# Attention scores: reciprocal and high part behind the own exponential, low part behind the next maximum; gates behind it too; head norms' first step on GpSimd

## The chip, the cores and the metric

The kernel runs on one core of a Trainium2 chip, as one program. The time is the device time of an execution in microseconds (us); before the change it was 1285.83, 1288.74 and 1289.24 us in three runs, median 1288.74. The profile is of one further execution, recorded by the hardware profiler. Engines are named as the profile names them: PE (TensorE, matrix multiplies; PEld its weight loads), DVE (VectorE), ACT (ScalarE), POOL (GpSimd) and SP (SyncE, which here only issues DMAs; SPq is its queue). L1075 and the like are lines of the kernel.

## The reference

One step of a two-layer model of width 1024 on 256 prompt tokens and 1024 latent tokens. Layer 0 mixes tokens with gated linear attention (GLA), layer 1 with grouped-query attention; the change touches layer 1. Everything is 32-bit.

```
proj = h @ w_in                      # h: modulated rms_norm of x
q, k, v, gate = split(proj)          # 8 query heads, 2 kv heads of 128
q, k = rms_norm(q, qn), rms_norm(k, kn)          # per head: "head norms"
q, k = rope_2d(q), rope_2d(k)                    # latent tokens only
s = q @ k.T * 128 ** -0.5            # latents see 1024 + 256 cached keys, the prompt its own 256
p = softmax(s)                       # maximum, exponential, divide by the sum
o = p @ v
y = (o * silu(gate)) @ w_out
x = x + gt * y
```

## The kernel before

**Number format.** Products of 32-bit values are made on PE from fp16 pairs: each operand is scaled by a power of two and split into a high part (the value rounded to fp16) and a low part (the rest), and `mm3` (L132) issues three matmuls for a product: high x high, high x low, low x high. So each matrix that goes into a product takes two elementwise passes, one for each part.

**Stages.** Of the profiled span of 1282 us the GLA layer takes the first 620 or so; until about 735 follows its output projection, with the second layer's norm, keys (`key_tile`) and first queries; `attention` runs until about 1180, and `att_out`, the last projection, ends the program.

**Attention.** `steps` holds ten tiles (p, c): kv half p (four query heads each) and a block c of 256 tokens; c = 0 is the prompt with 256 keys, c = 1 to 4 are latent blocks with 1280 keys. A tile has four heads and each head two scores j = 0, 1 of 128 queries, so there are 80 scores, 64 of them against 1280 keys. `scores` issues, for one score: the matmuls S (L1072, PE, into one of two PSUM tiles), the maximum smx (L1075, DVE), its scaled negative snb (L1077, ACT), and the exponential p with the sum sden beside it (L1080, ACT). `rest` turns p into what PE takes: the reciprocal srec of the sum (L1096, DVE), the same scaled, srec2 (L1098, DVE), the high part of p divided by the sum (L1101, POOL, "hi" below), the low part (L1102, DVE, "lo"), both in a tile phl, and a DMA transpose phl to PT (L1103, issued on SP). `values` multiplies PT with the values two heads later (L132, mm<-PT,vh and mm<-PT,vl), then multiplies by the gate (L1126, DVE, qk) and stores. Beside the scores, `query` and `query_rest` make the queries of coming tiles, one projection in every two heads: `head_norm` squares and sums on ACT (L919, hssq), then `rstd` takes hrsa = hssq/128 + eps (L121, DVE) and its power -1/2, hrs (L123, POOL), and DVE multiplies (L922); `rope` is eight POOL multiplies (L933) and two of DVE (L935, L936); a split and a DMA transpose follow (L946, L947, L950). `gateT` makes the gates of two heads: a projection on PE and silu, which is a tanh on ACT (ls, L275) and one DVE operation (gx, L277).

**Order.** A scheduler orders each engine's instructions by a simulated run before the program is built; on the chip each engine works through its list in that order. `issue_after(x)` makes what is issued under it come behind instruction x in that order. Before the change `scores` ends with `rest(last)`: the whole `rest` of the score before, all of reciprocal, hi, lo and transpose, is issued behind the maximum of the score just issued.

**Buffers.** p and phl have two buffers each, PT three, S two. So hi of a score waits until the transpose has read phl of two scores before, and an exponential waits until lo has read p of two scores before.

**End of attention.** Behind the last scores the output row of the first block, OUT[0], is brought back (`out2_load`) and split (`out2_prep`: two maxima L1211, a power of two by way of PE, then four splits L1218, L1219), the gate vector is folded into the output weights (L799, POOL), the first output tile is issued (`out_tile`), and the last two heads' `values` come last. `att_out` does the same for the other four blocks.

Of the kernel before, what the change touches and what calls it, by code (L numbers as in the profile page):

```python
# [7 lines left out]
F16 = mybir.dt.float16  # L8
F32 = mybir.dt.float32
# [3 lines left out]
ALU = mybir.AluOpType  # L13
# [4 lines left out]
P = 128  # L18
D = 1024
KT = D // P  # L20
TP, TS = 256, 1024
# [3 lines left out]
PAST = 256  # L25
GH, DK, DV, RANK = 4, 128, 256, 16
GQ, GV = GH * DK, GH * DV
HD, AH, KVH = 128, 8, 2
EPS = 1e-6
# [19 lines left out]
OUT = (1, 0, 2, 3, 4)  # L49
# [8 lines left out]
class K:  # L58
# [55 lines left out]
        return o  # L114


    def rstd(self, ssq, n, tag):
        nc = self.nc
        w = ssq.shape[1]
        a = self.t(self.sm, [P, w], F32, tag + "a")  # L120
        nc.vector.tensor_scalar(a, ssq, 1.0 / n, EPS, ALU.mult, ALU.add)  # L121
        r = self.t(self.sm, [P, w], F32, tag)
        nc.gpsimd.tensor_tensor(r, a, self.mhalf[:, 0:w], ALU.pow)  # L123
        return r
# [788 lines left out]
    def head_norm(self, x, g, out):  # L913
        nc = self.nc
        n = x.shape[1]
        ssq = self.t(self.sm, [P, n], F32, "hssq")
        junk = self.t(self.hw, [P, HD], F32, "hjunk", bufs=1)
        for j in range(n):
            nc.scalar.activation(junk, x[:, j, :], AF.Square, accum_out=ssq[:, j : j + 1])  # L919
        r = self.rstd(ssq, HD, "hrs")  # L920
        for j in range(n):
            nc.vector.scalar_tensor_tensor(out[:, j, :], x[:, j, :], r[:, j : j + 1], g, ALU.mult, ALU.mult)  # L922

# [134 lines left out]

    def scores(self, h, c, j, q, PT):
        nc = self.nc  # L1060
        kv = h // (AH // KVH)
        nk = 256 if c == 0 else TS + PAST
        k0 = 10 * P if c == 0 else 0
        S = (self.S0 or self.t(self.ps, [P, 1536], F32, "S"))[:, 0:nk]
        self.S0 = None
        qh, ql = (q[:, h % 4 // 2, m, h % 2, :] for m in range(2))
        a = 0
        while a < nk:
            n = min(512, nk - a)
            kh, kl = (t[:, kv, k0 + a : k0 + a + n] for t in (self.kTh, self.kTl))  # L1070
            for m, (x, y) in enumerate(((qh, kh), (qh, kl), (ql, kh))):
                nc.tensor.matmul(S[:, a : a + n], x, y, start=m == 0, stop=m == 2)  # L1072
            a += n
        mx = self.t(self.sm, [P, 1], F32, "smx")
        last = nc.vector.tensor_reduce(mx, S, AX.X, ALU.max).ins  # L1075
        nb = self.t(self.sm, [P, 1], F32, "snb")
        nc.scalar.activation(nb, mx, AF.Copy, scale=self.nsexp)  # L1077
        p = self.t(self.sp, [P, TS + PAST], F32, "p")[:, 0:nk]
        den = self.t(self.sm, [P, 1], F32, "sden")
        nc.scalar.activation(p, S, AF.Exp, scale=self.sexp, bias=nb, accum_out=den)  # L1080
        self.rest(last)
        self.last = last
        self.put_off = p, den, PT, j, nk


    def rest(self, after=None):
        if self.put_off is None:
            return
        if after is not None:
            with self.tc.issue_after(after):  # L1090
                return self.rest()
        nc = self.nc
        p, den, PT, j, nk = self.put_off
        self.put_off = None
        r = self.t(self.sm, [P, 1], F32, "srec")
        nc.vector.reciprocal(r, den)  # L1096
        r2 = self.t(self.sm, [P, 1], F32, "srec2")
        nc.vector.tensor_scalar(r2, r, 2.0 ** 14, None, ALU.mult)  # L1098
        parts = self.t(self.sp, [P, 2 * (TS + PAST)], F16, "phl")[:, 0 : 2 * nk]
        hi, lo = parts[:, 0:nk], parts[:, nk:]  # L1100
        nc.gpsimd.tensor_scalar(hi, p, r, 2.0 ** 14, ALU.mult, ALU.mult)  # L1101
        nc.vector.scalar_tensor_tensor(lo, p, r2, hi, ALU.mult, ALU.subtract)  # L1102
        nc.sync.dma_start_transpose(PT[:, 0 : 2 * nk // P, j * P : j * P + P], parts)  # L1103


    def gateT(self, h, c, w, inv):
# [2 lines left out]
        ps = self.bank("mm")[:, 0:256]  # L1109
        self.mm3(ps, lambda k: (hi[:, k, g0 : g0 + HD], lo[:, k, g0 : g0 + HD]), lambda k: self.hT(k, 256 * c, 256))  # L1110
        half, inv = inv[h % 4 // 2]
        return self.silu_raw(ps, half, 256), inv

    def values(self, h, c, PT, g):
        nc = self.nc
# [41 lines left out]
    def attention(self, wo):  # L1157
# [3 lines left out]
        for n, (p, c) in enumerate(self.steps):  # L1161
# [6 lines left out]
            for e in range(4):  # L1168
                h = 4 * p + e
                if later:  # L1170
                    self.nc.sync.dma_start(*later.pop(0))
                PT = self.t(self.sp, [P, 20, 256], F16, "PT", bufs=3)
                self.scores(h, c, 0, q[(p, c, 0)], PT)
                if e % 2 == 0:
                    self.query()
# [19 lines left out]
        self.fold_gate(1, o0[2] + [inv for _, inv in self.o1], gt)  # L1195
        wo[:] = [(*o0[0:2], 512)] + [(*w, 256) for w, _ in self.o1]
        self.out_tile(OUT[0], 0, self.t(self.sp, [P, TS + PAST], F32, "p")[:, 0:D], wo)
        for t in pend:
            self.values(*t, g.pop(t[0]))

# [3 lines left out]
        return og  # L1204

    def out2_prep(self, og, parts):
        nc = self.nc
        hi, lo = parts
        mx = self.t(self.small, [P, 2], F32, "wmx")
        for j in range(2):  # L1210
            nc.vector.tensor_reduce(  # L1211
# [1 line left out]
            )  # L1213
        m = self.t(self.small, [P, 1], F32, "wm1")
        nc.vector.tensor_tensor(m, mx[:, 0:1], mx[:, 1:2], ALU.max)
        s, inv = self.pow2(m)
        for k in range(0, AH, 4):
            nc.scalar.activation(hi[:, k : k + 4], og[:, k : k + 4], AF.Copy, scale=s)  # L1218
            nc.vector.scalar_tensor_tensor(  # L1219
# [15 lines left out]
    def att_out(self, wo):  # L1235
        w = self.wtile(2)
        for n, c in enumerate(OUT):
            if n + 1 < 5:
                nxt = self.out2_prep(self.out2_load(OUT[n + 1]), [t[:, :, 256 * (n % 2) : 256 * (n % 2) + 256] for t in w[0:2]])
            for j in range(n == 0, 2):  # L1240
                x = self.t(self.xp, [P, D], F32, "xr")
                self.out_tile(c, j, x, wo, (512, 256, 256) if (n, j) == (4, 1) else (512, 512))
# [353 lines left out]
```

## Time and profile before

| what | us |
|---|---|
| runs | 1285.83, 1288.74, 1289.24 (median 1288.74) |
| profiled execution, whole | 1284.12 |
| profiled execution, span | 1282.3 |
| PE busy in the span | 1212.2 |
| DVE / ACT / POOL busy | 895.1 / 584.8 / 389.2 |
| PE busy from 735 to 1180 (attention) | 428.37 of 445 |
| DVE busy from 735 to 1180 | 327.95 of 445 |

The profiled execution is its own run: its time, 1284.12, is 4.6 us under the median, and the 1.8 us between it and the span lie around the recorded work. A row of a stretch ("740.00:760.00 20.00, 18.79 (x118) ...") gives a stretch of the span, its length, the busy time of PE, PEld, DVE, ACT and POOL with the number of instructions, the clock that PE was granted (1.00 is full), the share of the DMA engines and GB/s. A row of the timeline gives start, duration, engine, line, operation, and output<-input; in brackets the time that the engine stood idle just before and what released it. A row of waits gives what waited, for what, us in all, how often, and the longest.

### The profile page before, as it was taken

To read this page: it belongs to the slowest core of one execution; us is meant where nothing else is said; L and a number is where in the kernel's file an instruction comes from. 1 tells how busy PE (TensorE), PEld (TensorE's weight loads), DVE (VectorE), ACT (ScalarE), POOL (GpSimd) and SP (SyncE) were. 2 spreads that over 40 slices of the span, in tenths; PEclk is the share of its full clock that TensorE was granted. 3 is DMA by queue.
4 is the path that set the end of the run, shared out by engine and by line. 5 is a ranking of instruction groups with operands and counts; after the bars stand their busy time and mean duration, and the time that the engine had idled before them with its cause. 6 is when DMAs were issued, how large, how long until landed. Compare 5 with 4: busy or idle time off the path is not lost. (4 is left out here: it accounts for less than half of the span.)

```text
span 1282.3 us, 22586 instructions
## 1 busy us (share of the span) xinstructions
PE 1212.2 (95%) x8295; PEld 810.6 (63%) x8295; DVE 895.1 (70%) x2072; ACT 584.8 (46%) x1425; POOL 389.2 (30%) x617
## 2 busy tenths in 40 slices
PE   4799999999999988999899999999999999999998
PEld 2347666655565545667578757677666766766675
DVE  5645876776688888764487678877667587875652
ACT  3546555555476566420265554444445454441110
POOL 0222222332233324300034545453233245522000
PEclk9899999999999999999999999999999999999999
DMA  9511363653444436994933367768848647768532
GB/s 362 194 66 39 128 198 123 191 164 104 128 135 136 123 111 207 281 206 150 296 131 109 64 142 141 143 125 152 190 107 169 138 91 145 137 133 207 185 130 84
DMA packets 333792, 194.41 MB, mean 152 GB/s; under 512 B 229663, under 2 KB 318607, under 8 KB 332401
## 3 DMA queue, kind: packets, MB, share of 16 engines
q1 hardware_dynamic: 291616, 159.02, 49.0%
q10 hardware_dynamic: 42064, 33.95, 8.6%
q8 instruction: 65, 1.06, 0.3%
q14 instruction: 47, 0.38, 0.1%
HBM read 103.00 MB, written 33.83 MB: 107 GB/s over the span
## 5 line engine op out<-in xcount | busy, mean ns | idle before, releaser
L132 PEld LDWEIGHTS <-hT_hi 128*128 128x128 f16 x1920 | 187.4, 98 | 126.6 <-issue 12.7
L132 PE MATMUL mm<-whi,hT_hi 128*128 128x512 f16 (+1 forms) x560 | 195.5, 349 | 4.0 <-ACT gx L541 2.8
L132 PE MATMUL mm<-wlo,hT_hi 128*128 128x512 f16 (+1 forms) x560 | 195.6, 349 | 0.0
L132 PE MATMUL mm<-whi,hT_lo 128*128 128x512 f16 (+1 forms) x560 | 195.4, 349 | 0.0
L132 PEld LDWEIGHTS <-whi 128*128 128x128 f16 x1408 | 137.9, 98 | 59.0 <-issue 6.2
L132 PE MATMUL mm<-hT_hi,whi 128*128 128x256 f16 (+1 forms) x512 | 153.4, 302 | 3.5 <-POOL hT_hi L416 2.9
L1101 POOL TENSOR_SCALAR phl<-p,srec 128x1280 f16<-128x1280 f32 (+1 forms) x80 | 99.8, 1248 | 186.5 <-DVE srec L1096 119.9
L132 PE MATMUL mm<-hT_lo,whi 128*128 128x256 f16 (+1 forms) x512 | 153.9, 301 | 0.2 <-DVE hT_lo L417 0.2
L132 PE MATMUL mm<-hT_hi,wlo 128*128 128x256 f16 (+1 forms) x512 | 153.7, 301 | 0.0
L1102 DVE SCALAR_TENSOR_TENSOR phl<-p,srec,phl 128x1280 f16<-128x1280 f32 (+1 forms) x80 | 107.6, 1345 | 49.7 <-POOL phl L1101 49.4
L132 PEld LDWEIGHTS <-hT_lo 128*128 128x128 f16 x960 | 94.3, 98 | 62.8 <-issue 1.9
L1072 PE MATMUL S<-kT,wst 128*128 128x512 f16 (+1 forms) x624 | 121.5, 338 | 5.0 <-ACT p L1080 5.0
L132 PE MATMUL mm<-PT,vh 128*128 128x256 f16 x672 | 114.3, 275 | 11.3 <-DMA PT<-phl 8.8
L1080 ACT ACTIVATE p<-S,snb,sexp 128x1280 f32<-128x1280 f32 (+1 forms) x80 | 99.7, 1247 | 30.2 <-DVE srec L1096 10.7
L1075 DVE TENSOR_REDUCE smx<-S 128x1 f32<-128x1280 f32 (+1 forms) x80 | 101.6, 1269 | 16.7 <-PE S L1072 16.7
L1072 PEld LDWEIGHTS <-wst 128*128 128x128 f16 x624 | 61.0, 98 | 56.7 <-issue 5.7
L132 PE MATMUL mm<-PT,vl 128*128 128x256 f16 x336 | 92.4, 275 | 0.0
L132 PEld LDWEIGHTS <-wlo 128*128 128x128 f16 x704 | 69.1, 98 | 29.9 <-issue 1.4
L1077 ACT ACTIVATE snb<-smx,nsexp 128x1 f32<-128x1 f32 x80 | 23.4, 293 | 133.1 <-DVE smx L1075 127.8
L132 PEld LDWEIGHTS <-vh 128*128 128x128 f16 x672 | 65.6, 99 | 23.0 <-issue 10.4
L933 POOL TENSOR_TENSOR rope<-hx,ropet 128x64 f32<-128x64 f32 x160 | 70.3, 468 | 9.2 <-DVE hx L936 5.6
L154 DVE TENSOR_REDUCE wmx<-wst 128x1 f32<-128x512 f32 x96 | 60.4, 676 | 9.0 <-DMA wst<-in_gla_w_in 5.7
(353 smaller groups left out, 2500.9 us busy)
## 6 DMA issues: line engine op xcount, KB each, us to landing
wada<-in_w_ada SPq DMA_DIRECT2D x13, 1024.0 KB
wst<-in_gla_w_in SPq DMA_DIRECT2D x12, 1024.0 KB
wst<-in_att_w_in SPq DMA_DIRECT2D x10, 1024.0 KB
xr<-x_d SPq DMA_DIRECT2D x15, 512.0 KB
og_d<-qk ACTq DMA_DIRECT2D x40, 128.0 KB
wst<-og_d SPq DMA_DIRECT2D x5, 1024.0 KB
out<-xr ACTq DMA_DIRECT2D x17, 256.0 KB
x<-in_x_sample SPq DMA_DIRECT2D x8, 512.0 KB
```

Source lines behind the costliest of these rows:

```text
L132: self.nc.tensor.matmul(out, a, b, start=k == 0 and j == 0, stop=k == n - 1 and j == 2)
L154: nc.vector.tensor_reduce(mx[:, j : j + 1], st[:, 2 * j : 2 * j + 2, :], AX.XY, ALU.max, apply_absolute_value=True)
L933: nc.gpsimd.tensor_tensor(tv[:, h, :, w, :], xv[:, h, :, 1 - w, :], sn[:, :, w, :], ALU.mult)
L1072: nc.tensor.matmul(S[:, a : a + n], x, y, start=m == 0, stop=m == 2)
L1075: last = nc.vector.tensor_reduce(mx, S, AX.X, ALU.max).ins
L1077: nc.scalar.activation(nb, mx, AF.Copy, scale=self.nsexp)
L1080: nc.scalar.activation(p, S, AF.Exp, scale=self.sexp, bias=nb, accum_out=den)
L1101: nc.gpsimd.tensor_scalar(hi, p, r, 2.0 ** 14, ALU.mult, ALU.mult)
L1102: nc.vector.scalar_tensor_tensor(lo, p, r2, hi, ALU.mult, ALU.subtract)
```

## The change

Four things change.

1. `rstd` takes an engine; `head_norm` has its first step (hrsa, L121) done on GpSimd, in all 50 head norms.
2. `rest` is cut in two. The new `high` issues reciprocal, srec2 and hi, and is called at the end of `scores` for the score's own p, with no `issue_after`; `rest`, still behind the next maximum, issues lo and the transpose alone. The last tile (n = 9, `tail`) keeps the old order: there `rest` calls `high` first.
3. In `gateT` the silu is issued behind the last maximum (`issue_after(self.last)`).
4. `out2_prep` is cut in `out2_scale` (maxima and power of two) and `out2_parts` (splits). The second block's row, OUT[1], is loaded and scaled in `attention` ahead of the last two heads' `values`; before, that was done in `att_out`.

```diff
--- before.py
+++ after.py
@@ -114,11 +114,11 @@
         return o
 
 
-    def rstd(self, ssq, n, tag):
+    def rstd(self, ssq, n, tag, eng=None):
         nc = self.nc
         w = ssq.shape[1]
         a = self.t(self.sm, [P, w], F32, tag + "a")
-        nc.vector.tensor_scalar(a, ssq, 1.0 / n, EPS, ALU.mult, ALU.add)
+        (eng or nc.vector).tensor_scalar(a, ssq, 1.0 / n, EPS, ALU.mult, ALU.add)
         r = self.t(self.sm, [P, w], F32, tag)
         nc.gpsimd.tensor_tensor(r, a, self.mhalf[:, 0:w], ALU.pow)
         return r
@@ -917,7 +917,7 @@
         junk = self.t(self.hw, [P, HD], F32, "hjunk", bufs=1)
         for j in range(n):
             nc.scalar.activation(junk, x[:, j, :], AF.Square, accum_out=ssq[:, j : j + 1])
-        r = self.rstd(ssq, HD, "hrs")
+        r = self.rstd(ssq, HD, "hrs", nc.gpsimd)
         for j in range(n):
             nc.vector.scalar_tensor_tensor(out[:, j, :], x[:, j, :], r[:, j : j + 1], g, ALU.mult, ALU.mult)
 
@@ -1081,6 +1081,20 @@
         self.rest(last)
         self.last = last
         self.put_off = p, den, PT, j, nk
+        if not self.tail:
+            self.high()
+
+
+    def high(self):
+        nc = self.nc
+        p, den, *to, nk = self.put_off
+        r = self.t(self.sm, [P, 1], F32, "srec")
+        nc.vector.reciprocal(r, den)
+        r2 = self.t(self.sm, [P, 1], F32, "srec2")
+        nc.vector.tensor_scalar(r2, r, 2.0 ** 14, None, ALU.mult)
+        parts = self.t(self.sp, [P, 2 * (TS + PAST)], F16, "phl")[:, 0 : 2 * nk]
+        nc.gpsimd.tensor_scalar(parts[:, 0:nk], p, r, 2.0 ** 14, ALU.mult, ALU.mult)
+        self.put_off = p, r2, parts, *to, nk
 
 
     def rest(self, after=None):
@@ -1090,15 +1104,11 @@
             with self.tc.issue_after(after):
                 return self.rest()
         nc = self.nc
-        p, den, PT, j, nk = self.put_off
+        if len(self.put_off) == 5:
+            self.high()
+        p, r2, parts, PT, j, nk = self.put_off
         self.put_off = None
-        r = self.t(self.sm, [P, 1], F32, "srec")
-        nc.vector.reciprocal(r, den)
-        r2 = self.t(self.sm, [P, 1], F32, "srec2")
-        nc.vector.tensor_scalar(r2, r, 2.0 ** 14, None, ALU.mult)
-        parts = self.t(self.sp, [P, 2 * (TS + PAST)], F16, "phl")[:, 0 : 2 * nk]
         hi, lo = parts[:, 0:nk], parts[:, nk:]
-        nc.gpsimd.tensor_scalar(hi, p, r, 2.0 ** 14, ALU.mult, ALU.mult)
         nc.vector.scalar_tensor_tensor(lo, p, r2, hi, ALU.mult, ALU.subtract)
         nc.sync.dma_start_transpose(PT[:, 0 : 2 * nk // P, j * P : j * P + P], parts)
 
@@ -1109,7 +1119,8 @@
         ps = self.bank("mm")[:, 0:256]
         self.mm3(ps, lambda k: (hi[:, k, g0 : g0 + HD], lo[:, k, g0 : g0 + HD]), lambda k: self.hT(k, 256 * c, 256))
         half, inv = inv[h % 4 // 2]
-        return self.silu_raw(ps, half, 256), inv
+        with self.tc.issue_after(self.last):
+            return self.silu_raw(ps, half, 256), inv
 
     def values(self, h, c, PT, g):
         nc = self.nc
@@ -1170,6 +1181,7 @@
                 if later:
                     self.nc.sync.dma_start(*later.pop(0))
                 PT = self.t(self.sp, [P, 20, 256], F16, "PT", bufs=3)
+                self.tail = n == len(self.steps) - 1
                 self.scores(h, c, 0, q[(p, c, 0)], PT)
                 if e % 2 == 0:
                     self.query()
@@ -1195,6 +1207,8 @@
         self.fold_gate(1, o0[2] + [inv for _, inv in self.o1], gt)
         wo[:] = [(*o0[0:2], 512)] + [(*w, 256) for w, _ in self.o1]
         self.out_tile(OUT[0], 0, self.t(self.sp, [P, TS + PAST], F32, "p")[:, 0:D], wo)
+        row = self.out2_load(OUT[1])
+        self.second = row, *self.out2_scale(row)
         for t in pend:
             self.values(*t, g.pop(t[0]))
 
@@ -1204,8 +1218,10 @@
         return og
 
     def out2_prep(self, og, parts):
-        nc = self.nc
-        hi, lo = parts
+        return self.out2_parts(og, *self.out2_scale(og), parts)
+
+    def out2_scale(self, og):
+        nc = self.nc
         mx = self.t(self.small, [P, 2], F32, "wmx")
         for j in range(2):
             nc.vector.tensor_reduce(
@@ -1213,7 +1229,11 @@
             )
         m = self.t(self.small, [P, 1], F32, "wm1")
         nc.vector.tensor_tensor(m, mx[:, 0:1], mx[:, 1:2], ALU.max)
-        s, inv = self.pow2(m)
+        return self.pow2(m)
+
+    def out2_parts(self, og, s, inv, parts):
+        nc = self.nc
+        hi, lo = parts
         for k in range(0, AH, 4):
             nc.scalar.activation(hi[:, k : k + 4], og[:, k : k + 4], AF.Copy, scale=s)
             nc.vector.scalar_tensor_tensor(
@@ -1236,7 +1256,8 @@
         w = self.wtile(2)
         for n, c in enumerate(OUT):
             if n + 1 < 5:
-                nxt = self.out2_prep(self.out2_load(OUT[n + 1]), [t[:, :, 256 * (n % 2) : 256 * (n % 2) + 256] for t in w[0:2]])
+                to = [t[:, :, 256 * (n % 2) : 256 * (n % 2) + 256] for t in w[0:2]]
+                nxt = self.out2_prep(self.out2_load(OUT[n + 1]), to) if n else self.out2_parts(*self.second, to)
             for j in range(n == 0, 2):
                 x = self.t(self.xp, [P, D], F32, "xr")
                 self.out_tile(c, j, x, wo, (512, 256, 256) if (n, j) == (4, 1) else (512, 512))
```

On DVE, around two maxima in the middle of attention (the first maximum of each listing is of the same score: S_10375 before is S_10381 of the change; the number in a name is only a count). Before:

```order
L1075 TENSOR_REDUCE smx_10385<-S_10375 128x1
L1096 RECIPROCAL srec_10392<-sden_10306 128x1
L1098 TENSOR_SCALAR srec_2404_10394<-srec_10392 128x1
L1102 SCALAR_TENSOR_TENSOR phl_10396<-p_10305,srec_2404_10394,phl_10396 128x1280
L121 TENSOR_SCALAR hrsa_10432<-hssq_10428 128x2
L1075 TENSOR_REDUCE smx_10459<-S_10449 128x1
L1096 RECIPROCAL srec_10466<-sden_10390 128x1
L121 TENSOR_SCALAR hrsa_10537<-hssq_10533 128x2
L922 SCALAR_TENSOR_TENSOR hx_2406_10400<-hx_2406_10400,hrs_10434,qn_7570 128x128 x2
L1098 TENSOR_SCALAR srec_2420_10468<-srec_10466 128x1
L1102 SCALAR_TENSOR_TENSOR phl_10470<-p_10389,srec_2420_10468,phl_10470 128x1280
```

With the change:

```order
L1075 TENSOR_REDUCE smx_10391<-S_10381 128x1
L1112 SCALAR_TENSOR_TENSOR phl_10320<-p_10311,srec_2392_10318,phl_10320 128x1280
L1092 RECIPROCAL srec_10400<-sden_10396 128x1
L1094 TENSOR_SCALAR srec_2407_10402<-srec_10400 128x1
L1075 TENSOR_REDUCE smx_10465<-S_10455 128x1
L1112 SCALAR_TENSOR_TENSOR phl_10404<-p_10395,srec_2407_10402,phl_10404 128x1280
L922 SCALAR_TENSOR_TENSOR hx_2409_10406<-hx_2409_10406,hrs_10440,qn_7570 128x128 x2
L922 SCALAR_TENSOR_TENSOR hx_2409_10406<-hx_2409_10406,hrs_10545,qn_7570 128x128 x2
L1137 SCALAR_TENSOR_TENSOR qk_7_82<-mm_10480,inv_g_2054_8506,gx_10349 128x256
L1092 RECIPROCAL srec_10474<-sden_10470 128x1
```

Before, every maximum has a reciprocal and srec2 of the score before behind it and then that score's lo; two hrsa lie between. With the change lo stands directly behind the maximum, its reciprocal came ahead of that maximum, and behind lo stands the reciprocal of the score whose maximum was just taken: srec_10400 belongs to smx_10391. The reciprocal of the next score, srec_10474, has a low part, four hx and one qk ahead of it.

On POOL at the same place, before:

```order
L1101 TENSOR_SCALAR phl_10396<-p_10305,srec_10392 128x1280
L123 TENSOR_TENSOR hrs_10434<-hrsa_10432,mhalf_85 128x2
L1101 TENSOR_SCALAR phl_10470<-p_10389,srec_10466 128x1280
L123 TENSOR_TENSOR hrs_10539<-hrsa_10537,mhalf_85 128x2
L933 TENSOR_TENSOR rope_10438<-hx_2406_10400,ropet_7568 128x2x32 x4
L1101 TENSOR_SCALAR phl_10529<-p_10463,srec_10525 128x1280
```

With the change:

```order
L1096 TENSOR_SCALAR phl_10404<-p_10395,srec_10400 128x1280
L121 TENSOR_SCALAR hrsa_10438<-hssq_10434 128x2
L123 TENSOR_TENSOR hrs_10440<-hrsa_10438,mhalf_85 128x2
L121 TENSOR_SCALAR hrsa_10543<-hssq_10539 128x2
L123 TENSOR_TENSOR hrs_10545<-hrsa_10543,mhalf_85 128x2
L933 TENSOR_TENSOR rope_10444<-hx_2409_10406,ropet_7568 128x2x32 x4
L1096 TENSOR_SCALAR phl_10478<-p_10469,srec_10474 128x1280
```

The two hrs of a query projection stood apart with a hi between them; now both stand behind the hi, each with its hrsa directly ahead, and all four ahead of the first rope.

On DVE at the entry to the last tile (smx_14205 before is smx_14211 of the change: the first score of tile n = 9). Before:

```order
L1075 TENSOR_REDUCE smx_14205<-S_14195 128x1
L1096 RECIPROCAL srec_14212<-sden_14126 128x1
L1098 TENSOR_SCALAR srec_3188_14214<-srec_14212 128x1
L1075 TENSOR_REDUCE smx_14230<-S_14220 128x1
L1102 SCALAR_TENSOR_TENSOR phl_14216<-p_14125,srec_3188_14214,phl_14216 128x1280
L1096 RECIPROCAL srec_14237<-sden_14210 128x1
L1126 SCALAR_TENSOR_TENSOR qk_7_82<-mm_14245,inv_g_2622_11538,gx_14163 128x256
```

With the change:

```order
L1075 TENSOR_REDUCE smx_14211<-S_14201 128x1
L1112 SCALAR_TENSOR_TENSOR phl_14140<-p_14131,srec_3176_14138,phl_14140 128x1280
L1075 TENSOR_REDUCE smx_14230<-S_14220 128x1
L1092 RECIPROCAL srec_14237<-sden_14216 128x1
L1094 TENSOR_SCALAR srec_3196_14239<-srec_14237 128x1
L1137 SCALAR_TENSOR_TENSOR qk_7_82<-mm_14245,inv_g_2625_11544,gx_14169 128x256
L1112 SCALAR_TENSOR_TENSOR phl_14241<-p_14215,srec_3196_14239,phl_14241 128x1280
```

Before, the low part of tile 8's last score (phl_14216) stood behind two maxima of tile 9 and behind its own reciprocal; now it stands behind one maximum (phl_14140), and its reciprocal has gone ahead of that. From the second score of the tile on the old order holds.

## The prediction

> **What bounds the kernel now.** I read the work by stretches first, then what PE waits for in attention, then the timeline at those waits, and the groups of instructions for durations. A row of a stretch has start:end, length, then PE, PEld, DVE, ACT and POOL busy, PE's clock, DMA share and GB/s.
>
> ```profile
> 735.00:1180.00 445.00, 428.37 (x3060) 299.18 (x3058) 327.95 (x624) 203.62 (x509) 186.06 (x238) 1.00 0.73 145
> 820.00:840.00 20.00, 20.00 (x139) 13.33 (x138) 15.20 (x26) 10.65 (x26) 10.21 (x11) 1.00 0.71 138
> 840.00:860.00 20.00, 20.00 (x145) 13.92 (x143) 16.07 (x27) 8.96 (x23) 8.83 (x12) 1.00 0.72 142
> ```
>
> In attention, the stage changed, PE is busy for 428.37 of 445 us. In the body of a run of tiles it has no gap: 20.00 of 20.00. So the change can give back only what PE idles, 445 - 428.37 = 16.6 us, and that lies in a few stretches:
>
> ```profile
> 740.00:760.00 20.00, 18.79 (x118) 11.35 (x117) 15.91 (x29) 11.27 (x27) 11.19 (x14) 1.00 0.54 113
> 760.00:780.00 20.00, 16.86 (x131) 12.51 (x130) 16.66 (x31) 10.49 (x25) 11.62 (x14) 1.00 0.80 148
> 920.00:940.00 20.00, 17.37 (x137) 13.08 (x135) 11.28 (x34) 7.50 (x26) 7.22 (x14) 1.00 0.80 155
> 980.00:1000.00 20.00, 18.17 (x145) 14.01 (x144) 15.28 (x30) 11.19 (x27) 6.94 (x6) 1.00 0.86 160
> 1000.00:1020.00 20.00, 19.48 (x150) 14.40 (x149) 11.49 (x35) 8.34 (x29) 7.71 (x15) 1.00 0.66 133
> 1060.00:1080.00 20.00, 18.34 (x133) 12.60 (x131) 17.11 (x32) 9.59 (x22) 11.60 (x14) 1.00 0.81 149
> 1120.00:1140.00 20.00, 17.02 (x115) 11.77 (x113) 17.57 (x24) 9.45 (x17) 6.50 (x5) 0.91 0.74 146
> 1140.00:1160.00 20.00, 17.62 (x139) 13.21 (x138) 15.36 (x26) 8.94 (x16) 4.20 (x4) 1.00 0.78 147
> ```
>
> PE's idle time by these rows: start of attention 1.21 + 3.14 = 4.35; change to the prompt tile (920) 2.63; start of the second half (980 to 1020) 1.83 + 0.52 = 2.35; 1060 1.66; the last tile 2.98 + 2.38 = 5.36. Together 16.35 of the 16.6. What ends these waits:
>
> ```profile
> PE mm L132 <- DMA PT<-phl: 8.8, 7, 2.6
> PE S L1072 <- ACT p L1080: 5.0, 4, 1.8
> PE mm L132 <- DVE ropet L1219: 2.4, 1, 2.4
> DVE phl L1102 <- POOL phl L1101: 49.4, 48, 3.3
> POOL phl L1101 <- DVE srec L1096: 119.9, 38, 6.2
> ```
>
> PE waits for a score's transposed parts (8.8 us) or for the exponential that frees its PSUM tile (5.0). Both stand at the end of one chain: maximum, exponential, reciprocal, hi, lo, transpose. The last two rows show the loose link: POOL stands 119.9 us waiting for a reciprocal that DVE issues only behind the next maximum, and then DVE stands 49.4 us waiting for POOL. That is time of DVE and POOL, and costs only where PE waits.
>
> **The change part by part.** *Reciprocal, srec2 and hi behind the own exponential.* Nothing is removed: each score keeps its six steps. What moves shows best at the last tile's entry:
>
> ```profile
> 1124.15 1.48 DVE L1075 TENSOR_REDUCE smx<-S 128x1 f32<-128x1280 f32 x1
> 1125.55 0.15 DVE L1096 RECIPROCAL srec<-sden 128x1 f32<-128x1 f32 x1
> 1125.85 1.33 POOL L1101 TENSOR_SCALAR phl<-p,srec 128x1280 f16<-128x1280 f32 x1 [4.36 <-DVE srec L1096]
> 1127.89 1.54 DVE L1102 SCALAR_TENSOR_TENSOR phl<-p,srec,phl 128x1280 f16<-128x1280 f32 x1
> 1129.46 3.39 SPq L1103 DMA_TRANSPOSE PT<-phl  x1
> 1131.11 1.78 PE L1072 MATMUL S<-kT,wst 128*128 128x512 f16 x9 [0.64 <-ACT p L1080]
> 1134.97 0.38 PE L132 MATMUL mm<-PT,vh 128*128 128x256 f16 x2 [2.07 <-DMA PT<-phl]
> 1135.00:1138.00 3.00, 3.00 (x20) 2.37 (x21) 3.00 (x3) 0.33 (x3) 1.32 (x1) 0.70 1.09 204
> 1138.00:1141.00 3.00, 3.00 (x23) 2.38 (x20) 1.57 (x6) 1.51 (x2) 1.33 (x1) 0.73 0.54 49
> ```
>
> POOL was free for 4.36 us before its reciprocal came. With the change hi is done by then, and lo can start where the reciprocal stood, at 1125.55 instead of 1127.89: the transpose is issued 1127.89 - 1125.55 = 2.3 us earlier, which covers the wait of 2.07 and pulls the exponentials behind it. Behind that wait PE's clock shows 0.70 and 0.73 for 3 us each: 3 x 0.30 + 3 x 0.27 = 1.7 us of work lost though PE counts as busy. I take the tile's recovery as 4 of its 5.36 (about 1.1 stays: from its second score on the old order holds) and 1.5 of the clock.
>
> [...] This case's trace shows the dip just behind the wait.
>
> The other places:
>
> ```profile
> 917.12 5.62 SPq L1103 DMA_TRANSPOSE PT<-phl  x1
> 924.98 1.33 POOL L1101 TENSOR_SCALAR phl<-p,srec 128x1280 f16<-128x1280 f32 x1 [6.14 <-DMA PT<-phl]
> 926.35 1.55 DVE L1102 SCALAR_TENSOR_TENSOR phl<-p,srec,phl 128x1280 f16<-128x1280 f32 x1 [3.32 <-POOL phl L1101]
> 933.07 0.38 PE L132 MATMUL mm<-PT,vh 128*128 128x256 f16 x2 [2.63 <-DMA PT<-phl]
> ```
>
> At 924.98 hi does not wait for a reciprocal, but 6.14 us for a phl buffer, held by a transpose of 5.62 us that shares the DMA engines with the gate weights. But the scores ahead of it were two steps late too: each gives up its hi of 1.33 between maximum and lo, so the transpose of 917 starts at least 1.33 earlier, and the next follows. Bounds 0 (the transpose is set by the traffic) and 2.63; I take 2.0, nearer the upper end, since the shift comes before the traffic. The clock of the stretch stayed at 1.00 (row of 920), so nothing of a clock is counted here.
>
> At 980 to 1020 weight loads make the transposes slow in the same way: bounds 0 and 2.35, taken 1.5. At 1060: bounds 0 and 1.66; in the same stretch DVE is busy for 17.11 of 20, the fullest of the body, so I take 0.5. At the start (4.35) the first three waits belong to scores with nothing ahead of them, and the new order puts four hx ahead of the third reciprocal: bounds 0 and 3, taken 1.5. The body of the tiles gives nothing, since PE is full there. Sum: 5.5 + 2.0 + 1.5 + 0.5 + 1.5 = 11.0.
>
> *What the early reciprocal costs.* DVE works in order, so a reciprocal whose sum is not there holds back the maximum behind it.
>
> ```profile
> L1102 DVE SCALAR_TENSOR_TENSOR phl<-p,srec,phl 128x1280 f16<-128x1280 f32 x64 | 99.7, 1557 | 46.2 <-POOL phl L1101 46.0
> L1077 ACT ACTIVATE snb<-smx,nsexp 128x1 f32<-128x1 f32 x80 | 23.4, 293 | 133.1 <-DVE smx L1075 127.8 <-DVE srec L1096 5.3
> 1126.04 1.42 ACT L1080 ACTIVATE p<-S,snb,sexp 128x1280 f32<-128x1280 f32 x1
> 1127.35 0.19 ACT L1080 ACTIVATION_READ_ACCUMULATOR p<-S,snb,sexp 128x1 f32 x1
> L936 DVE TENSOR_TENSOR hx<-hx,rope 128x256 f32<-128x256 f32 x28 | 20.6, 735 | 0.0
> L121 DVE TENSOR_SCALAR hrsa<-hssq 128x2 f32<-128x2 f32 x38 | 6.3, 168 | 27.8 <-ACT hjunk L919 27.8
> ```
>
> From maximum to sum it is 0.29 + 1.42 + 0.19 = 1.90 us on ACT; lo covers 1.56 of it, so at most 0.34 us is lost in each score that has no more between. Against that DVE no longer waits for hi: 49.4 us over 80 scores is 0.62 each. I take 0 in the body.
>
> *Head norms.* In attention 38 hrsa leave DVE, 38 x 0.168 = 6.3 us, and the 27.8 us that DVE stood ahead of them. On POOL none is seen; bounds from the nearest rows:
>
> ```profile
> L588 POOL COPY eb<-ep 128x4 f32<-128x4 f32 x40 | 13.3, 332 | 18.4 <-ACT ep L582 17.6 <-ACT ls L560 0.5
> L123 POOL TENSOR_TENSOR hrs<-hrsa,mhalf 128x2 f32<-128x2 f32 x50 | 37.1, 744 | 72.6 <-DVE hrsa L121 72.4
> ```
>
> Between 0.33 and 0.74 us; 0.4, since it is a plain multiply and add like the copy. 38 x 0.4 = 15 us on an engine that has 445 - 186 free. POOL's wait for the squares now holds hi behind it, up to 0.7 us a norm; lo is not due until the next maximum. I allow 1 us over the kernel, and 1 us at the end, where the second block's row (maxima and power of two) now stands on DVE ahead of the last two lo's; that it saves work in `att_out` gives nothing, PE being full there. *Gates behind the maximum:* they move two DVE operations of 0.4 us behind maxima: 0, as long as their PSUM tile is not wanted sooner.
>
> The sum: 11 - 2 = 9 us. The profiled execution goes from 1284.1 to 1275; the median stands 4.6 above that execution, so 1288.7 - 9 = 1280.
>
> **The rivals.** *The transitions stay.* At 924.98 POOL waits for a transpose, not for a reciprocal; if traffic sets all waits up to 1100, only part of the last tile is won, 0 to 3.8 us: about 1287. For it: five of the seven places have weight loads running beside them. Against: at 1125 the chain is plainly late by its order. *All is won.* 14 us and more, up to 16.6 + 1.7 = 18.3: 1271 to 1274. Against it: the start, and the old order in the last tile.
>
> *DVE becomes the bound: slower.* Mechanism: in the body, per two heads, DVE's operations and its waits for the exponential must fit in PE's period.
>
> ```profile
> 800.00 1.48 DVE L1075 TENSOR_REDUCE smx<-S 128x1 f32<-128x1280 f32 x1
> 823.46 1.48 DVE L1075 TENSOR_REDUCE smx<-S 128x1 f32<-128x1280 f32 x1
> 825.36 1.44 DVE L936 TENSOR_TENSOR hx<-hx,rope 128x256 f32<-128x256 f32 x1
> ```
>
> The two maxima are a period of 23.46 us apart (four scores and a query projection). DVE is busy for 15.20 to 16.07 of 20 us in the body, so for 17.8 to 18.9 of a period; about 5 us are free, 1.25 a score. Lost would be up to 0.34 a score for the exponential, and what hi beside DVE costs: L936 takes 0.735 in the mean and 1.44 here, beside POOL; if every operation with two tiles in SBUF (lo above all, 1.56) stretched by as much as L936 does, 0.7, the loss would be 1.04 and the body still fit. It decides from 1.25; with 0.2 us over that on 60 scores it is 12 us, less 5.5 won at the end: about 1295. For it: hi now runs beside DVE's work, where before DVE stood waiting for it. Against it: lo's mean is 1.557, beside the 1.54 and 1.55 of the rows above, so the long operation is not stretched today.
>
> [...]
>
> **How the numbers follow.** Forecast, 4 to 14 us won: 0.58, range 1275 to 1285. Transitions stay: 0.22. All won: 0.06. DVE the bound: 0.14. A measurement here tells about 0.3% from no change, 3.9 us: faster is below 1284.9, slower above 1292.6. Faster is 0.58 + 0.06 = 0.64; same 0.22; slower 0.14. The range 1271 to 1291 takes in all won and transitions that stay, and leaves out the slower case and what lies beyond the bounds.
>
> **What would show it.** Right: PE's idle time from 735 to 1180 falls from 16.6 to about 6; DVE's wait for POOL's hi falls from 49.4 to below 15; no wait of PE for PT over 1 us at the last tile's entry, and no dip of the clock behind it; the body stays at 20.00 of 20. Hrsa on POOL shows about 0.4 us. Wrong: gaps of PE in the body ended by the exponential (DVE the bound); the waits at 760, 933 and 990 unchanged (traffic); new waits of PE at 1150 to 1180, behind the second row's maxima.

## The result and the profile after

The changed kernel takes 1279.49 us in the median of ten runs, 1276.43 to 1286.28; beside it the kernel before took 1288.88, 1285.83 to 1291.97. The ratio is 0.994 with a 95% interval of 0.9922 to 0.9958: 7.7 us faster by the ratio, 9.4 by the medians. Run again beside other kernels it gave 0.9952 (0.9934 to 0.9969), so 6 to 8 us is the fair size. Of all runs here one, of e5 below, was slow: 1590.46 us; it is in that row's median and not in its ratio.

The profiled execution spans 1277.5 us, 4.8 less than the 1282.3 before. The stretches of attention, in the same order as before (start:end, length, PE, PEld, DVE, ACT and POOL busy, PE's clock, DMA share, GB/s):

```profile
735.00:1180.00 445.00, 435.73 (x3129) 304.97 (x3128) 326.58 (x601) 208.69 (x518) 206.48 (x283) 1.00 0.75 150
740.00:760.00 20.00, 17.77 (x113) 10.88 (x112) 13.66 (x23) 11.41 (x32) 10.26 (x15) 1.00 0.54 132
760.00:780.00 20.00, 18.18 (x125) 11.95 (x124) 17.36 (x30) 10.33 (x25) 12.49 (x19) 1.00 0.83 152
920.00:940.00 20.00, 20.00 (x162) 15.64 (x160) 10.79 (x26) 7.78 (x25) 7.74 (x15) 1.00 0.80 138
980.00:1000.00 20.00, 19.89 (x154) 14.85 (x153) 14.64 (x26) 10.89 (x25) 8.96 (x9) 1.00 0.99 172
1060.00:1080.00 20.00, 19.82 (x141) 13.46 (x140) 16.25 (x29) 8.79 (x18) 11.93 (x17) 1.00 0.81 156
1120.00:1140.00 20.00, 19.43 (x148) 14.11 (x147) 18.09 (x26) 8.59 (x17) 5.33 (x4) 1.00 0.67 129
1140.00:1160.00 20.00, 18.73 (x151) 14.43 (x150) 15.40 (x26) 9.90 (x16) 12.14 (x11) 1.00 0.96 218
1160.00:1180.00 20.00, 18.32 (x127) 12.03 (x125) 10.66 (x20) 2.66 (x3) 2.91 (x2) 1.00 0.89 219
```

PE's idle time in attention falls from 16.6 to 445 - 435.73 = 9.3 us. Counted from the first maximum to the last, which lie elsewhere in the two executions, it falls from 416.33 - 399.88 = 16.5 to 408.27 - 400.68 = 7.6 us. At 920 it is gone (2.63 to 0), at 980 nearly so (1.83 to 0.11), at 1060 too (1.66 to 0.18), and in 1120 to 1160 it falls from 5.36 to 1.84. At the start it stays: 2.23 + 1.82 = 4.05, after 4.35. And 1.68 us appear at 1160 to 1180, where there were none: behind the last maximum PE now waits 0.7 us for a PT and 1.0 us for the first output tile (p, L811).

PE's waits there, and the row of all maxima after and before (first and last start):

```profile
PE S L1072 <- ACT p L1080: 4.1, 4, 1.3
PE mm L132 <- DVE gx L277: 1.3, 1, 1.3
PE mm L132 <- DMA PT<-phl: 1.1, 2, 0.7
PE S L132 <- DVE p L811: 1.0, 1, 1.0
...
L1075 DVE TENSOR_REDUCE smx<-S x80: 410/1480/1492, 744.9 to 1153.2; 128x1 f32<-128x1280 f32 x64, 128x1 f32<-128x256 f32 x16
```

```profile
L1075 DVE TENSOR_REDUCE smx<-S x80: 407/1479/1493, 741.1 to 1157.4; 128x1 f32<-128x1280 f32 x64, 128x1 f32<-128x256 f32 x16
```

The waits for PT fell from 8.8 to 1.1 us; those for the exponential from 5.0 to 4.1 only. From the first maximum to the last it was 1157.4 - 741.1 = 416.3 us and is 1153.2 - 744.9 = 408.3: 8.0 us won in attention. That the span shows 4.8 is because attention begins 3.8 us later. Most of that lies ahead of the change, as the last matmuls of the GLA layer show, before and after:

```profile
L673 PE MATMUL U<-Sc,qe x10: 379/380/454, 503.5 to 600.2; 128*128 128x256 f32 x10
```

```profile
L673 PE MATMUL U<-Sc,qe x10: 379/380/382, 507.8 to 603.5; 128*128 128x256 f32 x10
```

They start 3.3 us apart in a stage that the change does not touch. In the other profiles below this stage ends anywhere from 599.7 to 606.3; the profiled execution before was one of the quick ones. So places are compared by distances within attention, not by the spans.

### The profile page after: what moved, and what is told of

Its sections match the earlier page's. It is cut to its first block, busy times and chain, and to the rows that moved or that the text cites. A ratio compares the mean times of both kernels' runs of the same rounds, so it can differ in the third digit from the quotient of the medians.

```text
span 1277.5 us, 22607 instructions
## 1 busy us (share of the span) xinstructions
PE 1210.1 (95%) x8295; PEld 808.3 (63%) x8295; DVE 884.7 (69%) x2022; ACT 585.3 (46%) x1425; POOL 410.0 (32%) x667
## 5 line engine op out<-in xcount | busy, mean ns | idle before, releaser
L1096 POOL TENSOR_SCALAR phl<-p,srec 128x1280 f16<-128x1280 f32 (+1 forms) x80 | 104.1, 1301 | 174.3 <-DVE srec L1092 95.4
L1075 DVE TENSOR_REDUCE smx<-S 128x1 f32<-128x1280 f32 (+1 forms) x80 | 101.6, 1271 | 44.3 <-PE S L1072 44.0
L1112 DVE SCALAR_TENSOR_TENSOR phl<-p,srec,phl 128x1280 f16<-128x1280 f32 (+1 forms) x80 | 106.7, 1333 | 23.6 <-POOL phl L1096 23.5
L1080 ACT ACTIVATE p<-S,snb,sexp 128x1280 f32<-128x1280 f32 (+1 forms) x80 | 99.7, 1246 | 13.3 <-DVE phl L1112 5.2
L1077 ACT ACTIVATE snb<-smx,nsexp 128x1 f32<-128x1 f32 x80 | 23.5, 293 | 116.6 <-DVE smx L1075 116.0
L933 POOL TENSOR_TENSOR rope<-hx,ropet 128x64 f32<-128x64 f32 x160 | 65.3, 436 | 19.1 <-DVE hx L936 10.5
L416 POOL TENSOR_SCALAR hT_hi<-h 128x256 f16<-128x256 f32 (+1 forms) x64 | 36.4, 577 | 96.2 <-ACT h L415 95.7
```

Source lines behind the costliest of these rows:

```text
L416: nc.gpsimd.tensor_scalar(hi, h, 1.0, 1.0, ALU.mult, ALU.mult)
L933: nc.gpsimd.tensor_tensor(tv[:, h, :, w, :], xv[:, h, :, 1 - w, :], sn[:, :, w, :], ALU.mult)
L1096: nc.gpsimd.tensor_scalar(parts[:, 0:nk], p, r, 2.0 ** 14, ALU.mult, ALU.mult)
```

## The experiments

All are edits of the changed kernel unless they say otherwise. "us" is the median; the ratio is to the kernel before, run beside it.

| run | us | ratio, 95% interval | first to last maximum | last maximum to end |
|---|---|---|---|---|
| before | | | 416.3 | 124.9 |
| changed | 1279.49 | 0.9940 (0.9922 to 0.9958) | 408.3 | 124.3 |
| e8, changed again | 1282.02 | 0.9952 (0.9934 to 0.9969) | 408.7 | 125.1 |
| e1, without early reciprocal and hi | 1290.55 | 1.0009 (0.9988 to 1.0030) | 418.4 | 124.5 |
| e2, early reciprocal and hi alone | 1287.65 | 0.9994 (0.9972 to 1.0016) | 409.7 | 127.7 |
| e3, head norms on DVE | 1283.76 | 0.9958 (0.9934 to 0.9983) | 409.8 | 125.3 |
| e4, gates free | 1280.44 | 0.9943 (0.9919 to 0.9967) | 409.9 | 125.7 |
| e5, second row late | 1285.33 | 0.9966 (0.9944 to 0.9987) | 409.0 | 131.0 |
| e6, no old order in the last tile | 1282.75 | 0.9952 (0.9930 to 0.9974) | 408.9 | 127.0 |
| e7a, DVE +0.67 us a score | 1297.93 | 1.0078 (1.0053 to 1.0104) | 422.5 | 126.0 |
| e7b, DVE +1.20 us a score | 1303.08 | 1.0115 (1.0087 to 1.0144) | 433.4 | 124.2 |
| e9, early reciprocal and second row | 1283.14 | 0.9964 (0.9944 to 0.9984) | 409.7 | 125.9 |
| e10, srec2 on POOL | 1281.29 | 0.9946 (0.9925 to 0.9967) | 411.2 | 121.0 |

The last two columns are of one profiled execution each. How many matmuls are left behind the last maximum depends on the order too (862 before, 842 in the changed kernel, 830 in e10), so the sum of the two columns is firmer than each: 541.2 before, 532.6 changed, 537.4 in e2, 535.6 in e9, 540.0 in e5.

**e1: without the early reciprocal**, all tiles in the old order:

```diff
-        if not self.tail:
-            self.high()
```

> The changed kernel, with reciprocal, srec2 and hi put back behind the next maximum in all tiles; head norms' first step on GpSimd, gates behind the maximum and the early second row stay. Theory (the early reciprocal carries the gain, the other three parts cost or give at most 1 us each): 1287 to 1290, PE's idle time in attention back at 15 to 18 us and a wait of about 2 us for PT at the last tile's entry. Rival (the gain comes from the other parts: DVE freed of the head norms' first step and of 27.8 us of standing ahead of it): 1279 to 1283.

1290.55, ratio 1.0009: nothing is left of the gain, and the intervals of this run and of the changed kernel do not meet. PE's idle time in attention is back, and so are the waits for PT:

```profile
735.00:1180.00 445.00, 426.39 (x3042) 297.44 (x3040) 333.93 (x591) 205.34 (x516) 197.43 (x284) 1.00 0.72 144
PE mm L132 <- DMA PT<-phl: 11.4, 7, 2.5
```

The early reciprocal is needed for the gain; the other three parts without it give nothing.

**e2: the early reciprocal alone** (the kernel before with that part only: hrsa on DVE, silu not tied, second row in the last projection).

```diff
-        r = self.rstd(ssq, HD, "hrs", nc.gpsimd)
+        r = self.rstd(ssq, HD, "hrs")
-        with self.tc.issue_after(self.last):
-            return self.silu_raw(ps, half, 256), inv
+        return self.silu_raw(ps, half, 256), inv
-        row = self.out2_load(OUT[1])
-        self.second = row, *self.out2_scale(row)
```

> The kernel before with the early reciprocal, srec2 and hi alone; head norms, gates and second row as before. Theory: 1277 to 1281, so as good as the whole change or up to 2 us better. Rival (the early reciprocal needs DVE freed of the head norms, or the gain comes from the other parts): 1284 to 1289.

1287.65, ratio 0.9994: the theory expected 1277 to 1281 and missed. In attention it does win, 416.3 to 409.7, 6.6 us; behind the last maximum it loses 2.8. PE's waits from there on in this kernel:

```profile
PE S L132 <- ACT whi L1235: 2.3, 1, 2.3
PE mm L132 <- DMA PT<-phl: 1.9, 1, 1.9
PE S L132 <- DVE wlo L1236: 0.7, 1, 0.7
```

The first and third are the second block's output row: PE comes to it before it is split, 2.3 + 0.7 = 3.0 us. The row's power of two goes by way of PE (mm<-ident,wm), and the split follows. Between that matmul and the row's first product PE had, in the kernel before, 15 matmuls of the first output tile left (1185.12 to 1188.41), and no such wait stood there. In e2 most of these stand earlier in PE's order: four are left, and from 1184.00 to 1186.29 PE waits. The gain of 6.6 less 2.8 would leave 3.8 us; the runs show 0.8 by the ratio and at most 3.6 by its interval, so some 3 us between this trace and the runs stay open.

**e5: the changed kernel with the second row late**, which asks for the same wait from the other side.

```diff
-        row = self.out2_load(OUT[1])
-        self.second = row, *self.out2_scale(row)
...
-                nxt = self.out2_prep(self.out2_load(OUT[n + 1]), to) if n else self.out2_parts(*self.second, to)
+                nxt = self.out2_prep(self.out2_load(OUT[n + 1]), to)
```

> The changed kernel with the second block's row loaded and scaled in the last projection, as before. Old reading (the early row gives nothing, PE being full there, and may cost 1 us): 1278 to 1280. Reading after the run with the early reciprocal alone (there the 6.6 us won between the first and the last maximum were followed by 3 us of PE waiting in the last projection for the second row's split): 1282 to 1284, with waits of PE for whi and wlo of about 3 us behind the last maximum that the changed kernel does not have.

1285.33, ratio 0.9966, 2 to 3 us behind the changed kernel by that one's two ratios. The old reading missed, and the waits are there again:

```profile
PE S L132 <- ACT whi L1236: 2.3, 1, 2.3
PE mm L132 <- DMA PT<-phl: 2.2, 1, 2.2
PE S L132 <- DVE wlo L1237: 0.7, 1, 0.7
```

Here too four matmuls are left ahead of the row's first product. Of the 131.0 us behind the last maximum, 6.7 more than in the changed kernel, these waits are 3.0; behind the waits of 2.2 and 2.3 the clock showed 0.66 and 0.68 for 3 us each, another 2.0.

**e9: early reciprocal and second row**, head norms and gates as before (the first two edits of e2).

> The kernel before with two parts: early reciprocal and early second row; head norms and gates as before. If the early reciprocal's 6.6 us in attention were lost again in the last projection for want of the second row: 2 to 4 us faster than the early reciprocal alone, ratio 0.996 to 0.998, and no PE wait for the second row's split; the remaining 3 to 5 us to the changed kernel would be the head norms'. If the early row only helps together with the head norms: ratio 0.999 to 1.001.

1283.14, ratio 0.9964, inside what the first reading expected: 3.9 us under the early reciprocal alone. The rest to the changed kernel, expected at 3 to 5 us, is 1.5 to 3.1 by its two ratios. Neither whi nor wlo is waited for any more:

```profile
PE S L132 <- DVE p L811: 2.2, 2, 1.3
PE mm L132 <- DMA PT<-phl: 0.8, 1, 0.8
PE mm L90 <- DVE wm L1230: 0.3, 1, 0.3
```

So these two parts are most of the change: the one wins 6.6 us in attention, the other keeps some 2 to 4 of them from being lost in the last projection. The 2 to 4 us rest on two pairs (e2 and e9, e5 and the changed kernel) whose intervals overlap; the waits of 3.0 us, in both traces that have the early reciprocal without the early row and in none of the ten with the row, carry the reading.

**e3: head norms' first step on DVE again** (the first edit of e2 alone).

> The changed kernel with the head norms' first step back on VectorE. Theory: within 1.5 us of the changed kernel (1278 to 1281), with DVE standing again some 20 to 30 us ahead of the step, hidden. Rival (head norms on GpSimd are what lets the reciprocals through): 1283 to 1288.

1283.76, ratio 0.9958 (0.9934 to 0.9983). The median lies 2.8 us over what the theory allowed, and at the bottom of the rival's range; the interval takes in the changed kernel's 0.9940 and 0.9952. In attention it is 409.8 after 408.3 and 408.7. A gain of 1 to 2 us from this part fits all of it; it is not told from nothing. DVE stood 9.8 us ahead of the step in attention (27.8 before), not the 20 to 30 that the theory expected.

**e4: gates free** (the second edit of e2 alone).

> The changed kernel with the gates' silu not tied to the last maximum. Theory: 0 within 1 us of the changed kernel (1278.5 to 1280.5). Rival (gates ahead of the maximum delay the chain by their 0.4 us each, twice in two heads): 2 to 5 us slower, 1281.5 to 1284.5, with PE waiting for the exponential in more places than the four of the changed kernel.

1280.44, ratio 0.9943: the gates' place makes no difference that can be measured, as the theory had it. The intervals alone would allow up to some 3 us, but the rival's sign is missing too: PE waits for the exponential in four places, as in the changed kernel.

**e6: the new order in the last tile too.**

```diff
-                self.tail = n == len(self.steps) - 1
+                self.tail = False
```

> The changed kernel with the early reciprocal and hi in the last tile too. If the old order is what leaves waits in the last tile (1.25 us in the 10 us before the last maximum, where the wait for hi behind lo shows on GpSimd): 1 to 2 us faster, 1277.5 to 1278.5. Rival (there the chain is held by the output row's split and by buffers): within 1 us, or slower by 1 to 3 where hi then lies beside lo and each waits for the other.

1282.75, ratio 0.9952: not faster, so the rival holds. From the first maximum to the last it takes 408.9 us, no less than the changed kernel (408.3 and 408.7), and behind it PE waits longer for the first output tile, 2.79 us after 1.03:

```profile
1171.53 3.80 PE L132 MATMUL S<-kept,ropet 128*128 128x256 f16 x22 [2.79 <-DVE p L811]
```

**e7a and e7b: VectorE loaded on purpose.** The predicted slower case was to decide from 1.25 us lost a score. A maximum over 512 or 1024 columns of p, whose result nobody uses, was added behind the reciprocal of 56 scores:

```diff
             self.high()
+            if nk > 256:
+                dm = self.t(self.sm, [P, 1], F32, "sdm", bufs=1)
+                nc.vector.tensor_reduce(dm, p[:, 0:512], AX.X, ALU.max)
```

> The changed kernel with one more VectorE operation in 56 scores, a maximum over 512 columns of p whose result nobody uses, behind the reciprocal; estimated from the row's maxima over 1024 columns (1.21 us) at 0.6 to 0.7 us each, 34 to 39 us in all. The prediction's slower case decides from 1.25 us a score lost on VectorE; if that point is right the body of the tiles stays at 20.00 of 20 and the time rises by 0 to 4 us, at the transitions. If VectorE is the bound already, or its slack is less than half of the stated one: 15 to 35 us slower.

> The same with 1024 columns, 1.2 us each, 67 us in all. By the stated point (1.25) this is just at the edge: 3 to 15 us slower with gaps of PE in the body. If VectorE has much more room: 0 to 3 us. If much less: 30 us and more.

The smaller one took 0.667 us each, 37 us in all, and the ratio went from 0.9940 to 1.0078: 17.8 us, or 16.2 from e8's ratio. The larger, 1.197 us each, went to 1.0115, 22.5 us (21.0). The stated point was wrong; where it fails is shown by the body of the tiles, 780 to 900. The stretch and DVE's waits in it, first of the kernel before, then of the changed one, then of e7a and e7b:

```profile
780.00:900.00 120.00, 120.00 (x862) 84.13 (x860) 93.00 (x161) 54.42 (x132) 53.59 (x62) 1.00 0.74 138
DVE phl L1102 <- POOL phl L1101: 16.1, 16, 1.3
DVE hrsa L121 <- ACT hjunk L919: 8.5, 5, 2.2
DVE smx L1075 <- PE S L1072: 0.7, 1, 0.7
```

```profile
780.00:900.00 120.00, 120.00 (x867) 84.59 (x865) 91.09 (x158) 57.76 (x134) 57.83 (x73) 1.00 0.77 141
DVE smx L1075 <- PE S L1072: 18.1, 10, 3.0
DVE phl L1112 <- POOL phl L1096: 1.4, 1, 1.4
```

```profile
780.00:900.00 120.00, 118.97 (x855) 83.32 (x854) 101.30 (x172) 53.35 (x131) 52.65 (x76) 1.00 0.72 134
DVE smx L1075 <- PE S L1072: 3.8, 3, 1.6
```

```profile
780.00:900.00 120.00, 114.43 (x799) 78.93 (x800) 107.05 (x161) 51.03 (x119) 49.09 (x72) 0.99 0.71 130
DVE smx L1075 <- PE S L1072: 0.7, 1, 0.7
```

DVE is busy for nearly the same time before and after, 93.0 and 91.1 us, and PE is full in both. But before, DVE stood 16.1 us for POOL's hi and 8.5 us for the head norms' squares and waited for PE's scores once, 0.7 us; after, it stands 18.1 us for them. The reading is that only a wait for PE is slack, and that in the other two work of DVE is already late. For the changed kernel the sums bear it out. With 0.67 us more a score, 20 of them in the stretch, 13.3 of the 18.1 us should be used up: 3.8 are left, and PE loses 1.0 of 120. With 1.20, 19 of them, 22.7 are asked for, 4.6 more than there is: PE loses 5.6. So the body does hold at 0.67 (nearly) and not at 1.20; 18.1 us over 20 scores put the point at about 0.9, not at 1.25. That the waits of the kernel before were no slack is argued, not shown: no run loads DVE there. The larger part of e7a's 17.8 us falls outside this stretch. At the start, for one, PE is busy for 33.20 of 40 us where the changed kernel has 17.77 + 18.18 = 35.95:

```profile
740.00:780.00 40.00, 33.20 (x211) 20.36 (x209) 33.86 (x56) 21.29 (x54) 18.94 (x29) 1.00 0.68 140
```

So 2.75 us are lost to six added operations, 4.0 us: at the start most of each added step is paid.

**e10: the other way, srec2 off VectorE.**

```diff
-        nc.vector.tensor_scalar(r2, r, 2.0 ** 14, None, ALU.mult)
         parts = ...
         nc.gpsimd.tensor_scalar(parts[:, 0:nk], p, r, 2.0 ** 14, ALU.mult, ALU.mult)
+        nc.gpsimd.tensor_scalar(r2, r, 2.0 ** 14, None, ALU.mult)
```

> The changed kernel with srec2 (80 x 0.149 = 11.9 us of VectorE in attention) on GpSimd, behind hi. If VectorE's time counts at the transitions (0.67 us more for a score made it 18 us slower, so about 0.4 us for each us of VectorE): 2 to 5 us faster than the changed kernel, 1275 to 1278, and VectorE's standing for PE's scores rises from 44 to above 50 us. Rival (the added GpSimd step lengthens the chain from hi to lo by its own 0.2 us, and nothing is won): within 1 us, or up to 2 us slower.

1281.29, ratio 0.9946: no better than the changed kernel, so the rival holds, though the slack did grow as expected:

```profile
DVE smx L1075 <- PE S L1072: 50.6, 31, 3.8
DVE phl L1112 <- POOL srec L1096: 13.0, 12, 1.7
DVE phl L1112 <- POOL phl L1095: 11.5, 7, 2.9
PE mm L132 <- DMA PT<-phl: 4.4, 4, 3.1
```

In attention DVE stands for PE 50.6 us after 44.0. Ahead of lo it waits 13.0 + 11.5 = 24.5 us for POOL, after 23.5: what it no longer waits for hi it waits for the moved step. PE waits 4.4 us for PT, after 1.1. More slack in the body bought nothing here; PE is full there already in the changed kernel, 120.00 of 120 us from 780 to 900. No kernel here beats the changed one by more than the measurement.

## Why the prediction was right, and where it was not

**Time and sign.** 1280 in 1271 to 1291, faster at 0.64; measured 1279.49. The likeliest case came true, and by its mechanism. In the profiled executions the places, forecast at 11.0, gave 16.5 - 7.6 = 8.9 us of idle time and the 1.7 of the clock, 10.6; behind the last maximum PE idles 1.2 us more (5.0 to 6.1), where 2 were charged in all. What was luck is the second row: charged as a cost, it kept 3.0 us of new waits away that the sum did not know of.

**The places.** PE's idle time, forecast 16.6 to about 6, came to 9.3. Won at 920: 2.63 (forecast 2.0). At 980 to 1020: 2.35 to 0.11 (forecast 1.5 won). At 1060: 1.66 to 0.18, all but won (forecast 0.5). The last tile: 5.36 to 1.84, 3.5 (forecast 4). The start: 0.3 (forecast 1.5). These stretches lie up to 3.8 us apart in the two executions; counted from tile to tile, the four places behind the start won 2.2, 2.0, 1.3 and 3.1. So the transitions gave more, the start and the last tile less. "The transitions stay" is refuted: the gate weights' loads are issued from 907.01 to 916.60 before and from 909.16 to 910.70 after, the DMA share from 920 to 940 is 0.80 in both, and PE's idle time there fell from 2.63 to 0. At 980 to 1020 no trace shows the weight loads that the 1.5 was reasoned from: the last piece of w_o is issued at 962.25 before and at 960.31 after, and the six transposes issued from 979.75 to 1004.07 before took 2.93 to 3.80 us, where the median of all 80 is 3.08.

**The step at the last tile's entry** was right in mechanism and size. The same place after:

```profile
1122.29 1.49 DVE L1075 TENSOR_REDUCE smx<-S 128x1 f32<-128x1280 f32 x1 [0.70 <-PE S L1072]
1123.70 1.54 DVE L1112 SCALAR_TENSOR_TENSOR phl<-p,srec,phl 128x1280 f16<-128x1280 f32 x1
1131.11 0.38 PE L132 MATMUL mm<-PT,vh 128*128 128x256 f16 x2 [0.57 <-DVE smx L1075]
```

Lo stands directly behind the first maximum, 1.41 us after its start; before it was 1127.89 - 1124.15 = 3.74. That is the forecast 2.3 us. PE's wait of 2.07 for PT is gone, and the clock of the stretch is 1.00 after 0.91. A slip in the working: of 5.36 less 4 about 1.4 stays, not 1.1; it was 1.84.

**DVE's wait for hi** was to fall below 15; it fell from 49.4 to 23.5 over attention, but to 1.4 in the body. The rest lies in the transitions, where POOL waits for a phl buffer and not for a reciprocal (18.1 us before). Over attention, after:

```profile
POOL phl L1096 <- DMA PT<-phl: 63.9, 19, 6.7
DVE phl L1112 <- POOL phl L1096: 23.5, 19, 3.0
```

**The early second row was mis-sized, and its sign was wrong.** The step said that the work it saves in the last projection "gives nothing, PE being full there", and charged 1 us. PE was full there only as long as matmuls of the first output tile were left behind the row's power of two, 15 before and four in e2 and e5: these two show 3.0 us of waits and 2 to 4 us of time without the row. The charge itself may be real: the wait for the first output tile (p, L811), 1.0 us in the changed kernel, stands in eight of the ten traces with the early row and in none of the three without. What the step overlooked: a stretch in which the bound engine is full says nothing about what comes once the work ahead of it is shorter or in another order.

**Head norms** were charged 1 us for POOL; e3 shows 1 to 2 us of gain or nothing. Its price was near the forecast one: 0.461 us in the mean (0.4 taken), though the usual one is 0.192:

```profile
L121 POOL TENSOR_SCALAR hrsa<-hssq x50: 191/192/1553, 666.1 to 1107.4; 128x2 f32<-128x2 f32 x50
```

**The slower case** did not come, but its point was wrong (e7a): free time was counted as span less busy time, 5 us in a period, without asking whom DVE waited for. With the right reading, about 0.9 a score, the prediction's upper loss of 1.04 lies beyond the point, and the chance of the slower case would have been higher. No run shows the 0.7 of it that stands for a stretched lo: in attention lo took 1.546 us in the mean with the change, 1.557 before.

## What to carry to other kernels

Idle time of an engine can be slack or lateness, so ask whom it waits for before counting it as free: the 18.1 us that DVE stood for PE in the changed kernel from 780 to 900 came down to 3.8 in e7a, where PE lost 1.0 of 120, and to 0.7 in e7b, where it lost 5.6; that time ended by a third engine is lateness is argued, not shown. Here, from 780 to 900, 24.6 us of waits ended by POOL and ACT became 18.1 ended by PE at nearly the same busy time. Both the order and the moved step have a part in it: there DVE waits 11.1 us for PE's scores in e2, which has the order alone, and 8.1 in e1, which has the head norms on POOL without it. Slack is room and not time won: over attention e1 shows 35.0 us of it after 16.7, and is no faster.

And when a change shortens or reorders a stage, look for the first load or split of the next stage that work on the bound engine had hidden: here its 3.0 us would have taken back nearly half of the gain.

## What the runs showed of the hardware that was not expected

**A hi that started beside a lo took longer.** A hi takes 1.33 us on POOL by itself. Two hi's of the changed kernel that start while a lo runs on DVE; below them one of the kernel before, which started 0.19 us ahead of L936 on DVE:

```profile
764.24 1.52 DVE L1112 SCALAR_TENSOR_TENSOR phl<-p,srec,phl 128x1280 f16<-128x1280 f32 x1
764.77 2.51 POOL L1096 TENSOR_SCALAR phl<-p,srec 128x1280 f16<-128x1280 f32 x1 [1.54 <-DMA PT<-phl]
...
973.96 1.54 DVE L1112 SCALAR_TENSOR_TENSOR phl<-p,srec,phl 128x1280 f16<-128x1280 f32 x1
973.97 2.65 POOL L1096 TENSOR_SCALAR phl<-p,srec 128x1280 f16<-128x1280 f32 x1 [0.65 <-DMA PT<-phl]
```

```profile
825.17 1.36 POOL L1101 TENSOR_SCALAR phl<-p,srec 128x1280 f16<-128x1280 f32 x1 [1.17 <-issue]
```

Beside lo, which came first, hi is longer by about the overlap: 0.99 us of overlap and 1.18 us more, 1.53 and 1.32 more; lo keeps its 1.52 to 1.54. In the third case hi came first and keeps 1.36, and it is L936, started at 825.36, that takes 1.44 (the row is in the prediction) where it takes 0.41 to 0.43 by itself. So in these rows the one that started first keeps its time and the other is longer; not in all, for the L936 at 758.43 before starts 0.11 us behind a hi and takes 0.41. A hi beside a maximum was not stretched: that at 772.95 before lies 1.29 us beside one and takes 1.33. What makes the difference, no run here shows. The prediction looked for a stretched lo and saw none; in these rows, where lo comes first, it is hi that is stretched. It cost little here, since only four of 64 hi's took over 2 us.

**PE's clock dipped behind some waits of over 2 us, and behind none shorter.** In the 13 profiles, from 735 to 1190 us, PE waited 46 times between 1.2 and 2.0 us, and the 3 us behind showed 1.00 every time; of 18 waits from 2.05 to 3.68 us nine had 0.52 to 0.71 behind them. Length alone does not decide: of these two in e7a, the stretch behind a wait of 3.29 us and that behind one of 3.46, the first shows 1.00 and the second 0.52.

```profile
777.71:780.71 3.00, 3.00 (x28) 2.70 (x29) 3.00 (x4) 1.80 (x3) 1.33 (x1) 1.00 0.92 174
1073.78:1076.78 3.00, 3.00 (x15) 2.15 (x16) 3.00 (x7) 0.27 (x1) 2.04 (x4) 0.52 1.13 205
```

The shortest wait with a dip was 2.05 us, in e9, with 0.66 in the 3 us behind it. What decides besides the length, no run here shows.
